# Rotary columns regrouped by halves of four maps, and differential scores in four row tiles of 32

## The chip, the cores and the metric

The kernel runs on one core of one Trainium2 chip. The metric is the device time of one execution in microseconds (us), as the median of several executions. Engines are named as in the profile: PE (TensorE, matmuls), PEld (its weight loads), DVE (VectorE), ACT (ScalarE), POOL (GpSimd) and SP (which issues the transfers from memory).

## The reference, cut to what matters

One decoder layer on 512 tokens of width 1024: a mixer (forgetting attention with 8 heads, and differential attention with rotary positions), cross-attention, a mixture of 32 experts, and a final norm. The part that the change touches is the differential attention. It has 4 heads with two maps each, and a map has 64 columns of query and 64 of key:

```python
def _rope(t, cos, sin):
    half = t.shape[-1] // 2
    t1, t2 = t[..., :half], t[..., half:]
    return jnp.concatenate([t1 * cos - t2 * sin, t2 * cos + t1 * sin], axis=-1)
...
        dq = _rope(dq.reshape(b, s, DIFF_HEADS, 2, HEAD_DIM), cos, sin)
        dk = _rope(dk.reshape(b, s, DIFF_HEADS, 2, HEAD_DIM), cos, sin)
...
        s1 = jnp.einsum('bhqd,bhkd->bhqk', q1[:, :, q0:qe], k1[:, :, :qe]).astype(jnp.float32) * scale
        s2 = jnp.einsum('bhqd,bhkd->bhqk', q2[:, :, q0:qe], k2[:, :, :qe]).astype(jnp.float32) * scale
        p1 = jax.nn.softmax(jnp.where(mask, s1, -jnp.inf), axis=-1)
        p2 = jax.nn.softmax(jnp.where(mask, s2, -jnp.inf), axis=-1)
        a = (p1 - lam * p2).astype(v.dtype)
```

## The kernel before, in words

Every float32 operand of a large matmul is split into a high and a low part (`split`, L174 to L176: an ACT copy to the high part, then a DVE subtraction for the low one), and a product takes three matmuls (high by high, low by high, high by low; L277 to L279).

The mixer is one loop over 24 iterations (L924 on). The first 16 are the forgetting attention (`Fox`, four pairs of heads by four blocks of 128 queries; block b sees 128(b+1) keys), the last 8 the differential attention (`Diff`, two groups g of four maps by four blocks). The order on each engine is that of the code (a manual schedule), and every engine works in order. An iteration does, in this order: the scores of its block on PE (`scores`), the maxima on DVE and the exponentials on ACT (`soft`), a projection unit on PE (`unit()`, 24 matmuls of 512 columns for a transposed one, some 5.5 us), the product with the values of the iteration before (`av`), the scaling (`combine`, DVE), the next half of a weight split (`W.more`), the transposes (`trans`, PE), and then the unit's evacuation `ev()` and the copies of the transposed probabilities out of PSUM (`copy`: the first of two on DVE, the second on ACT). In a Fox iteration `ev()` stands ahead of `copy`, in a Diff iteration behind it.

The rotary units (`rope_unit`) are the units of Fox iterations 6 to 9 (group 0) and 12 to 15 (group 1): query half 0, query half 1, key half 0, key half 1, of 128 columns each. A unit of before holds two whole maps. Its evacuation splits the raw result, multiplies it by the cosine, and puts a `rest` on the list `late`. `rest` runs in the next iteration behind the scores: two matmuls with a signed permutation matrix `swp` exchange the halves (L645, L646), DVE multiplies by the sine and adds, and the sum is split again.

PSUM banks come from rings (L67): two of tag "a" for units and for the exchange, four of tag "s" for scores, transposes and the key bias of a new pair (`prep`, at the end of iterations 3, 7 and 11), two of tag "y". A new tile takes the bank that was taken longest ago and waits for that tile's last reader. So the two score banks of a Fox iteration are as a rule those of the scores before. Behind a `prep` they are those of the transposes before, and a Diff iteration, which takes four banks for scores and two for transposes, has two of each.

The scores of a Diff block go by `qk_mm` (L536): two maps at a time, each on 64 rows of the array and into its own bank, so that two matmuls stand in the array side by side. Then the mask is added (L672).

Of the kernel before, what the change touches and what calls it, by code (L numbers as in the profile page):

```python
# [10 lines left out]
F32 = mybir.dt.float32  # L11
F32R = mybir.dt.float32r
# [3 lines left out]
OP = mybir.AluOpType  # L16
AX = mybir.AxisListType

P = 128
D = 1024  # L20
S = 512
# [17 lines left out]
def tile_hybrid_block(  # L39
# [5 lines left out]
    V, A, PE, G = nc.vector, nc.scalar, nc.tensor, nc.gpsimd  # L45
# [7 lines left out]
    c1 = wstack.enter_context(tc.tile_pool(name="c1", bufs=1))  # L53
    wk = wstack.enter_context(tc.tile_pool(name="wk", bufs=2))

    def page(shape, dt, name):
        return pgp.tile(list(shape), dt, name=name, tag="pg")
# [3 lines left out]
    def work(shape, dt, name, tag="w"):  # L61
        return wk.tile(list(shape), dt, name=name, tag=tag, bufs=bufs[tag])
# [10 lines left out]
    def bank(name, tag):  # L73
        return ps.tile([P, 512], F32, name=name, tag=tag, bufs={"a": 2, "s": 4, "y": 2}[tag])
# [41 lines left out]
    class Stream:  # L116
# [28 lines left out]
        def split(self, upto):  # L145

            while self.done < min(upto, 2 * len(self.spec)):
                i, j = divmod(self.done, 2)
                self.load(self.done + 1)
                _, k, n = self.spec[i]  # L150
                if j == 0:
                    self.hl[i] = [self.new.get((i, u), page)([P, k, n], F32R, f"w{u}{i}") for u in "hl"]
                hi, lo = self.hl[i]
                sl = slice(j * k // 2, (j + 1) * k // 2)
                n = k // 2 // 2 if self.done < 2 else k // 2
                for k0 in range(0, k // 2, n):
                    d = slice(sl.start + k0, sl.start + k0 + n)
                    split(hi[:, d], lo[:, d], self.raw[self.done][:, k0:k0 + n])
                self.done += 1
                self.load(self.done + 4)  # L160
# [51 lines left out]
    jp = c1.tile([P, P], F32, name="jp")  # L212
# [96 lines left out]
    def t_unit(chunk, j, evac, name):  # L309

        wh, wl = W.use(chunk, j)
        o = bank(f"{name}p{j}", "a")
        sl = slice(j * P, (j + 1) * P)
        gemm(o, KD, lambda k: wh[:, k, sl], lambda k: wl[:, k, sl], lambda k: hk(HH, k), lambda k: hk(HL, k))
        return lambda: evac(j, o)
# [113 lines left out]
    for u in range(NT):  # L429
        PE.matmul(pc[:, 8 * u:32], onesf if u else trif, logf[:, 0:NT - u].rearrange("p t c -> p (t c)"),  # L430
                  start=(u == 0), stop=(u == NT - 1), skip_group_check=True)
# [18 lines left out]
    rot = {}  # L450
# [4 lines left out]
    def rotary_angles():  # L455
        G.tensor_scalar(gcc, gcc, 0.125, None, op0=OP.mult)
        G.tensor_tensor(wr, wr, gfc[:, :, None].to_broadcast([P, KD, 36]), op=OP.mult)
        rot["sc"] = page([P, 16, P], F32, "rt")
        pf = tiny([P, NT], "pf")
        G.tensor_copy(pf, pos_i)  # L460
        ang = scratch(4)
        G.tensor_tensor(ang, pf[:, :, None].to_broadcast([P, NT, 32]), invf[:, None, :].to_broadcast([P, NT, 32]),
                        op=OP.mult)
        MAGIC = 1.5 * 2.0 ** 23
        pi_frac = Fraction(31415926535897932384626433832795028841971693993751, 10 ** 49)
        turn = pi_frac * 2
        k = scratch(0)
        G.tensor_scalar(k, ang, float(1 / turn), MAGIC, op0=OP.mult, op1=OP.add)
        G.tensor_scalar(k, k, -MAGIC, None, op0=OP.add)
        kh, kp = scratch(1), scratch(2)  # L470
        G.tensor_scalar(kh, k, 1024 * MAGIC, None, op0=OP.add)
        G.tensor_scalar(kh, kh, -1024 * MAGIC, None, op0=OP.add)
        G.tensor_tensor(k, k, kh, op=OP.subtract)
        rest = turn
        for i in range(4):
            p = cut(float(rest), 11 if i < 3 else 24)
            rest -= Fraction(p)
            for part in (kh, k):
                G.tensor_scalar(kp, part, p, None, op0=OP.mult)
                G.tensor_tensor(ang, ang, kp, op=OP.subtract)  # L480
        rot["ang"] = ang
# [55 lines left out]
    def qk_mm(banks, rows, d, j, q0, n):  # L537

        for u, w in ((0, 0), (0, 1), (1, 0)):
            for o, r0 in zip(banks, rows):  # L540
                r = slice(r0, r0 + 64)
                PE.matmul(o[:, 0:n], d[u][r, 0, j, q0:q0 + P], d[w][r, 1, j, 0:n], start=(u + w == 0), stop=False)

    class Fox:
# [15 lines left out]
        def scores(self):  # L560
            pr, b, n = self.pr, self.b, self.n
            d = fqk[pr // 2]
            self.banks = [bank(f"sf{pr}{b}{i}", "s") for i in range(2)]
            qk_mm(self.banks, [0, 64], d, pr % 2, b * P, n)
            for i in range(2):
                PE.matmul(self.banks[i][:, b * P:n], identb, maskb, start=False, stop=True)
# [51 lines left out]


    dqk = {}  # L620
    late = []
    swp = c1.tile([P, P], F32R, name="swp")

    def swap_matrix():
        for i in range(4):
            sl = slice(32 * i, 32 * i + 32)
            sg = 1.0 if i % 2 else -1.0
            V.tensor_scalar(swp[:, sl], jp[:, sl], 32.0 * sg, sg, op0=OP.is_equal, op1=OP.mult)


    def rope_unit(g, w, j):

        if g not in dqk:
            dqk[g] = [page([P, 2, 2, S], F32R, f"dqk{g}{u}") for u in "hl"]
        h, l = (t[:, w, j] for t in dqk[g])
        nm = f"r{g}{w}{j}"

        def evac(j, o):
            split(h, l, o)
            a1 = work([P, S], F32, nm + "a")  # L640
            V.tensor_tensor(a1, o, rot["cos"], op=OP.mult)

            def rest():
                sw = bank(nm + "s", "a")
                PE.matmul(sw, swp, h, start=True, stop=False)  # L645
                PE.matmul(sw, swp, l, start=False, stop=True)  # L646
                b1 = work([P, S], F32, nm + "b")
                V.tensor_tensor(b1, sw, rot["sin"], op=OP.mult)
                V.tensor_tensor(a1, a1, b1, op=OP.add)
                split(h, l, a1)  # L650

            late.append(rest)

        return t_unit((c_dq, c_dk)[w][g], j, evac, f"d{'qk'[w]}{g}")

# [2 lines left out]
    class Diff:  # L658
# [6 lines left out]
        def scores(self):  # L665
            g, b, n = self.g, self.b, self.n
            d = dqk[g]
            self.banks = [bank(f"sd{g}{b}{i}", "s") for i in range(4)]
            for j in range(2):
                qk_mm(self.banks[2 * j:2 * j + 2], [0, 64], d, j, b * P, n)  # L670
            for i in range(4):
                PE.matmul(self.banks[i][:, b * P:n], identb, maskb, start=False, stop=True)  # L672

# [240 lines left out]
    def unit():  # L914

        ev = None
        while ev is None:
            ev = units.pop()()
        return ev
# [4 lines left out]
    for n, it in enumerate(its):  # L924
        it.scores()
        it.soft()
        while late:
            late.pop(0)()
        fe = rows() if rows is not None else None
        ev = unit()  # L930
        if fe is not None:
            fe()
        fin2 = prev.av() if prev is not None else None
        if n == 1:
            swap_matrix()
        if n == 2:
            rotary_angles()
        if n == 3:
            rotary_tables()
        if n == 4:  # L940
            lam_calc()
        if n == 5:
            rotary_spread()
        if n == 7:
            dv = page([P, NT, 512], F32, "dv")
        it.combine()
        if fin is not None and isinstance(done, Diff):
            done.scale()
        W.more()
        if isinstance(it, Diff):  # L950
            ev()
            while late:
                late.pop(0)()
            ev = unit()
            W.more()
        it.trans()
        if isinstance(it, Diff):
            it.copy()
            ev()
        else:  # L960
            ev()
            it.copy()
        rows = fin
        if isinstance(it, Fox) and it.b == NT - 1 and it.pr < 3:
            Fox(it.pr + 1, 0).prep()
        if n == 15:
            YB["h"] = page([P, 4, S], F32R, "ybh")
            YB["l"] = page([P, 4, S], F32R, "ybl")
        done, prev, fin = prev, it, fin2
# [338 lines left out]
    for step in """T0 N0 U20 Q0 U21 K0 T1 N1 U30 U22 W Q1 S0 M0 K1 U23 U31 N2 T2 S1 P0 Q2 M1 U32 A0 U33 K2 T3 O0 N3 S2  # L1308
# [5 lines left out]
        f, t = step[0], int(step[1]) if len(step) > 1 else 0  # L1314
# [244 lines left out]
    for p in range(NE // 2):  # L1559
# [3 lines left out]
        h = []  # L1563
        for a in range(2):
            e = 2 * p + a
            sl = slice((2 * qi + a) * CAP, (2 * qi + a + 1) * CAP)
# [24 lines left out]
        late = more and qi == 1  # L1591
# [33 lines left out]
    def rows(o, t, j, first):  # L1625
        for u in range(2):
            PE.matmul(o, oh[:, t * P:(t + 1) * P], y2[:, u, j], start=first and u == 0, stop=(u == 1))  # L1627
# [150 lines left out]
```

## Time and profile before

| | |
|---|---|
| median of 3 runs | 1001.63 us (998.44 to 1002.61) |
| the profiled execution, its own time | 1002.39 us |
| its span, first to last instruction | 1000.7 us |
| PE busy | 960.4 us, 96% of the span |
| DVE busy, ACT busy | 473.9 us (47%), 308.7 us (31%) |
| mean granted PE clock, share of 2.4 GHz | 0.99 |
| the Fox iterations with rotary units | about 104 to 198 us from the start |
| the Diff iterations | about 189 to 297 us |
| the experts | about 500 to 985 us |

A matmul's record is longer than the distance to the next one, because matmuls overlap; for the cost on the path the distance between starts is read, not the duration. The same holds for DVE, whose records overlap by some 0.08 us.

### The profile page before, as it was taken

What the parts mean: (1) busy time and instruction counts of PE and PEld (TensorE: products, weight loads), DVE (VectorE), ACT (ScalarE), POOL (GpSimd) and SP (SyncE); (2) the same over time, 40 slices, a digit from 0 to 9 for tenths busy, and PEclk for the clock granted to TensorE, in tenths of its full rate; (3) what the DMA queues carried; (4) which work ended last, traced back from release to release, by engine and by line L of the source; (5) the groups of instructions that cost most, each with busy time, mean ns of one, the idle gap of its engine ahead of it and who ended that gap; (6) DMA issues with size and microseconds to landing.
All of it is one profiled execution on the core that took longest, in us unless ns stands there. A gap on an engine that the chain in (4) does not pass through costs nothing. (4 is left out here: it accounts for less than half of the span.)

```text
span 1000.7 us, 13844 instructions
## 1 busy us (share of the span) xinstructions
PE 960.4 (96%) x5494; PEld 639.7 (64%) x5495; DVE 473.9 (47%) x1023; ACT 308.7 (31%) x672; POOL 74.7 (7%) x189
## 2 busy tenths in 40 slices
PE   7999999999999999999799999999999999999985
PEld 6787688887878898998647446363453635436332
DVE  6555776857663657556722233433233242233335
ACT  5444444544443344435322112121111212102114
POOL 1840000001113000000200000000000000000003
PEclk9999999999999999999899999999999999999998
DMA  8211122122141337239399899999999999999902
GB/s 310 85 64 64 64 64 64 52 76 64 64 147 64 101 119 244 95 121 367 123 361 419 333 421 418 423 420 418 420 420 421 420 421 421 420 421 418 405 6 85
DMA packets 47862, 246.19 MB, mean 246 GB/s; under 512 B 4784, under 2 KB 12208, under 8 KB 23728
## 3 DMA queue, kind: packets, MB, share of 16 engines
q1 hardware_dynamic: 47648, 245.24, 62.0%
q8 instruction: 45, 0.74, 0.3%
q14 instruction: 25, 0.20, 0.1%
q10 hardware_dynamic: 144, 0.00, 0.0%
HBM read 243.13 MB, written 2.10 MB: 245 GB/s over the span
## 5 line engine op out<-in xcount | busy, mean ns | idle before, releaser
L1409 PE MATMUL gu<-gu,xg 128*64 128x512 f32 x960 | 210.5, 593 | 1.7 <-PEq L1478 1.6
L1409 PEld LDWEIGHTS gu<-gu,xg 128*64 128x64 f32 x960 | 72.9, 137 | 133.2 <-issue 123.1
L1431 PE MATMUL yd<-dn,A 128*64 128x512 f32 x472 | 110.4, 596 | 0.0
L1453 DVE TENSOR_TENSOR xr<-cb,xr 128x512 f32<-128x512 f32 x120 | 75.7, 684 | 50.8 <-PE cb L1449 50.6
L1414 DVE SCALAR_TENSOR_TENSOR A<-A,gu 128x256 f32<-128x256 f32 x32 | 13.5, 421 | 176.1 <-ACT A L1413 176.1
L176 DVE TENSOR_TENSOR wl<-wr,wh 128x1024 fp32r<-128x1024 f32 (+1 forms) x66 | 78.4, 1196 | 32.2 <-ACT wh L175 31.6
L1431 PEld LDWEIGHTS yd<-dn,A 128*64 128x64 f32 x472 | 34.9, 137 | 64.3 <-issue 63.4
L1413 ACT ACTIVATE A<-gu 128x256 f32<-128x256 f32 x32 | 12.3, 385 | 201.1 <-PE gu L1409 201.1
L175 ACT ACTIVATE wh<-wr 128x1024 fp32r<-128x1024 f32 (+1 forms) x66 | 67.0, 1026 | 7.4 <-DVE wr L142 6.4
L1449 PE MATMUL cb<-Y,ohT 128*128 128x512 f32 x240 | 67.4, 411 | 0.9
L1439 DVE SCALAR_TENSOR_TENSOR Y<-yd,ws,Y 128x512 fp32r<-128x512 f32 x32 | 23.9, 750 | 91.8 <-ACT Y L1438 89.9
L1237 PE MATMUL ga<-G,hnh 128*128 128x256 f32 x256 | 64.6, 290 | 0.2 <-DVE ge L1357 0.2
L1237 PE MATMUL ga<-G,hnl 128*128 128x256 f32 x256 | 62.7, 282 | 0.0
L1438 ACT ACTIVATE Y<-yd,ws 128x512 fp32r<-128x512 f32 x32 | 21.9, 687 | 126.9 <-PE yd L1431 126.9
L1449 PEld LDWEIGHTS cb<-Y,ohT 128*128 128x128 f32 x240 | 42.5, 191 | 12.6 <-DVE xr L1453 3.4
L1237 PEld LDWEIGHTS ga<-G,hnh 128*128 128x128 f32 x256 | 48.5, 190 | 3.1 <-issue 2.4
L1237 PEld LDWEIGHTS ga<-G,hnl 128*128 128x128 f32 x256 | 48.6, 190 | 0.6
L1383 ACT ACTIVATE xg<-ga,smc 128x256 f32<-128x256 f32 x64 | 29.9, 475 | 52.3 <-PE ga L1237 52.3
L277 PE MATMUL wop<-wh,mh 128*128 128x256 f32 x128 | 36.8, 287 | 2.0 <-DVE g L845 1.4
L278 PE MATMUL wop<-wl,mh 128*128 128x256 f32 x128 | 36.2, 283 | 0.0
L279 PE MATMUL wop<-wh,ml 128*128 128x256 f32 x128 | 36.2, 283 | 0.0
L1549 POOL MEMSET A<- 128x128 f32 x1 | 0.2, 206 | 438.2 <-PE pth L274 438.2
(609 smaller groups left out, 1888.5 us busy)
## 6 DMA issues: line engine op xcount, KB each, us to landing
gu<-in_w_gu_dram SPq DMA_DIRECT2D x120, 1024.0 KB, 11.0
dn<-in_w_dn_dram SPq DMA_DIRECT2D x55, 1024.0 KB, 16.2
wr<-in_w_inp_dram SPq DMA_DIRECT2D x40, 512.0 KB, 3.7
Z<-in_w_gu_dram SPq DMA_DIRECT2D x8, 1024.0 KB, 13.6
wr<-in_w_out_dram SPq DMA_DIRECT2D x8, 512.0 KB, 5.0
Z<-in_w_dn_dram SPq DMA_DIRECT2D x4, 1024.0 KB, 19.8
dn<-in_w_dn_dram SPq DMA_DIRECT2D x6, 512.0 KB, 12.8
x<-in_x_dram SPq DMA_DIRECT2D x2, 1024.0 KB, 11.5
```

The costliest lines, as they stand in the source:

```text
L175: A.activation(hi, src, AF.Copy)
L176: V.tensor_tensor(lo, src, hi.bitcast(F32), op=OP.subtract)
L277: PE.matmul(o, lh, rh, start=first, stop=False)
L278: PE.matmul(o, lh, rl, start=False, stop=False)
L279: PE.matmul(o, ll, rh, start=False, stop=last)
L1237: PE.matmul(o, CX[u, t // 2][:, t % 2, kb * P:(kb + 1) * P], GQ[q][:, t].rearrange("p e s -> p (e s)"), start=(first and u == "h"), stop=( ...
L1383: A.activation(XG[q][:, kb], o, AF.Copy, scale=gfc[:, kb:kb + 1])
L1409: PE.matmul(gu[64 * f:64 * f + 64, :], xg(2 * i + j), w[:, :, j, 256 * f:256 * f + 256], start=(i + j == 0), stop=(i + j == 4))
L1431: PE.matmul(y[j][64 * a:64 * a + 64, :], hT[a][:, f % 2, f // 2], w(a, f)[:, j, f % 2], start=(f == 0), stop=(f == 3))
L1439: V.scalar_tensor_tensor(yl[rows, j], y[j][rows], ws, yh[rows, j].bitcast(F32), op0=OP.mult, op1=OP.subtract)
L1449: PE.matmul(banks[j], oh[:, t * P:(t + 1) * P], y[u][:, j], start=(u == 0), stop=(u == 1))
L1453: V.tensor_tensor(xs, banks[j], xs, op=OP.add)
```

## The change

The host reorders the 1024 columns of the rotary query and key weights. Each chunk of 256 columns (four maps of 64) is laid out as the first 32 columns of the four maps, and then the second 32 columns of the four maps. A unit's 128 rows are then the first halves (j = 0) or the second halves (j = 1) of four maps, and the two halves that a rotation combines stand on the same rows of two units. The evacuation of unit 0 makes the products with cosine and sine and keeps them. That of unit 1 does the same, combines the two units, and splits the two results. `late`, `swp` and the matmuls with it are gone. A map now has 32 rows in each of two tiles. The scores run over the two halves j, over the three products, and over four maps, each on 32 rows of the array and into its own bank.

```diff
     dqk = {}
-    late = []
-    swp = c1.tile([P, P], F32R, name="swp")
...
+    rp = {}
...
         def evac(j, o):
-            split(h, l, o)
-            a1 = work([P, S], F32, nm + "a")
-            V.tensor_tensor(a1, o, rot["cos"], op=OP.mult)
-
-            def rest():
-                sw = bank(nm + "s", "a")
-                PE.matmul(sw, swp, h, start=True, stop=False)
-                PE.matmul(sw, swp, l, start=False, stop=True)
-                b1 = work([P, S], F32, nm + "b")
-                V.tensor_tensor(b1, sw, rot["sin"], op=OP.mult)
-                V.tensor_tensor(a1, a1, b1, op=OP.add)
-                split(h, l, a1)
-
-            late.append(rest)
+            c, s = (work([P, S], F32, nm + "cs"[i]) for i in range(2))
+            V.tensor_tensor(c, o, rot["cos"], op=OP.mult)
+            V.tensor_tensor(s, o, rot["sin"], op=OP.mult)
+            if j == 0:
+                rp[g, w] = c, s
+                return
+            c0, s0 = rp[g, w]
+            V.tensor_tensor(c0, c0, s, op=OP.subtract)
+            V.tensor_tensor(c, c, s0, op=OP.add)
+            for i, v in enumerate((c0, c)):
+                split(dqk[g][0][:, w, i], dqk[g][1][:, w, i], v)
...
             for j in range(2):
-                qk_mm(self.banks[2 * j:2 * j + 2], [0, 64], d, j, b * P, n)
+                for u, v in ((0, 0), (0, 1), (1, 0)):
+                    for i, o in enumerate(self.banks):
+                        r = slice(32 * i, 32 * i + 32)
+                        PE.matmul(o[:, 0:n], d[u][r, 0, j, b * P:b * P + P], d[v][r, 1, j, 0:n],
+                                  start=(j + u + v == 0), stop=False)
...
         it.soft()
-        while late:
-            late.pop(0)()
...
             ev()
-            while late:
-                late.pop(0)()
...
+    w2[:, 1536:2560] = w2[:, 1536:2560].reshape(D, 4, 4, 2, 32).transpose(0, 1, 3, 2, 4).reshape(D, 1024)
```

On DVE, at the end of Fox iteration 7 (pair 1, block 3, the unit `dq0p1`) and the start of iteration 8 the rows of before are these. `wl7` is the weight split, `pf130` the copy of the transposed probabilities, `S200` and `mx20` the next maxima.

```order
L176 TENSOR_TENSOR wl7_1208<-wr71_1049,wh7_1207 128x1024 [waits DMAHW2_49,Activation_49]
L176 TENSOR_TENSOR dqk0l_1171<-dq0p1_1259,dqk0h_1170 128x512 [waits Activation_49]
L641 TENSOR_TENSOR r001a_1311<-dq0p1_1259,rot_1113 128x512
L602 COPY pf130_1313<-tf130_1299 128x512 [waits PE_49]
L574 ISA S200_1334,mx20_1336<-sf200_1324,cb2_1317 128x128 [waits PE_49,Activation_49]
```

After:

```order
L176 TENSOR_TENSOR wl7_1203<-wr71_1044,wh7_1202 128x1024 [waits DMAHW2_49,Activation_49]
L631 TENSOR_TENSOR r001c_1296<-dq0p1_1246,rot_1108 128x512 [waits PE_49]
L632 TENSOR_TENSOR r001s_1297<-dq0p1_1246,rot_1108 128x512
L637 TENSOR_TENSOR r000c_1216<-r000c_1216,r001s_1297 128x512 [waits DVE_49]
L638 TENSOR_TENSOR r001c_1296<-r001c_1296,r000s_1217 128x512
L176 TENSOR_TENSOR dqk0l_1166<-r000c_1216,dqk0h_1165 128x512 [waits Activation_49]
L176 TENSOR_TENSOR dqk0l_1166<-r001c_1296,dqk0h_1165 128x512 [waits Activation_49]
L602 COPY pf130_1306<-tf130_1286 128x512 [waits PE_49]
L574 ISA S200_1327,mx20_1329<-sf200_1317,cb2_1310 128x128 [waits PE_49,Activation_49]
```

The copy `pf130` had two rotary operations between itself and the weight split, and now has six.

On PE, the scores of the second Diff block (iteration 17) began like this before; `sd010` to `sd013` are the four score banks:

```order
L542 MATMUL sd010_2224<-dqk0h_1170 128x256 [waits Activation_49]
L542 MATMUL sd011_2225<-dqk0h_1170 128x256 [waits Activation_49]
L542 MATMUL sd010_2224<-dqk0l_1171,dqk0h_1170 128x256
L542 MATMUL sd011_2225<-dqk0l_1171,dqk0h_1170 128x256
L542 MATMUL sd010_2224<-dqk0h_1170,dqk0l_1171 128x256
L542 MATMUL sd011_2225<-dqk0h_1170,dqk0l_1171 128x256
L542 MATMUL sd012_2226<-dqk0h_1170 128x256 [waits DVE_49]
L542 MATMUL sd013_2227<-dqk0h_1170 128x256 [waits Activation_49]
```

After:

```order
L661 MATMUL sd010_2191<-dqk0h_1165 128x256 [waits Activation_49]
L661 MATMUL sd011_2192<-dqk0h_1165 128x256 [waits Activation_49]
L661 MATMUL sd012_2193<-dqk0h_1165 128x256 [waits DVE_49]
L661 MATMUL sd013_2194<-dqk0h_1165 128x256 [waits Activation_49]
L661 MATMUL sd010_2191<-dqk0l_1166,dqk0h_1165 128x256
L661 MATMUL sd011_2192<-dqk0l_1166,dqk0h_1165 128x256
L661 MATMUL sd012_2193<-dqk0l_1166,dqk0h_1165 128x256
L661 MATMUL sd013_2194<-dqk0l_1166,dqk0h_1165 128x256
```

The matmuls that wait for the banks of the transposes before (`sd012` for a DVE copy, `sd013` for an ACT copy) stood in seventh and eighth place and now stand in third and fourth. There are 12 matmuls before the mask in a block of before, and 24 of after.

## Rows read from the trace of the kernel before

**Rows 1.** Busy time of each engine in stretches of the span, with clock and DMA.
```profile
core 0: us, PE busy (x) PEld busy (x) DVE busy (x) ACT busy (x) POOL busy (x), PEclk, DMA share, GB/s
198.00:290.00 92.00, 89.79 (x530) 74.42 (x527) 58.14 (x133) 43.84 (x114) 12.82 (x42) 1.00 0.26 86
...
580.00:620.00 40.00, 40.00 (x221) 20.97 (x221) 11.81 (x22) 6.72 (x14) 0.00 (x0) 1.00 1.02 420
```
**Rows 2.** Timeline around two exchanges: start, us, what, [idle before <-releaser].
```profile
112.83 0.48 PE L645 MATMUL r000s<-dqk0h,swp 128*128 128x512 f32 x1
...
113.63 0.19 PEld L277 LDWEIGHTS dq0p<-hh,wh 128*128 128x128 f32 x1 [0.41 <-DVE r000a L641]
...
131.20 0.48 PE L645 MATMUL r010s<-dqk0h,swp 128*128 128x512 f32 x1
...
131.75 0.39 PE L277 MATMUL dk0p<-hh,wh 128*128 128x512 f32 x1
```
**Rows 3.** Timeline, end of iteration 7 and scores of iteration 8.
```profile
120.56 0.69 DVE L176 TENSOR_TENSOR dqk0l<-dq0p,dqk0h 128x512 fp32r<-128x512 f32 x1
...
121.16 0.68 DVE L641 TENSOR_TENSOR r001a<-dq0p,rot 128x512 f32<-128x512 f32 x1
...
121.76 0.68 DVE L602 COPY pf<-tf 128x512 f32<-128x512 f32 x1
...
122.49 0.32 PE L542 MATMUL sf<-fqk1h 64*128 64x128 f32 x1 [0.30 <-DVE pf L602]
```
**Rows 4.** Timeline, end of iteration 15 and scores of iteration 16.
```profile
188.18 0.68 DVE L176 TENSOR_TENSOR dqk1l<-dk1p,dqk1h 128x512 fp32r<-128x512 f32 x1
...
190.11 0.18 PEld L542 LDWEIGHTS sd<-dqk0h 64*128 64x128 f32 x1 [0.28 <-DVE pf L602]
...
190.59 0.40 PE L672 MATMUL sd<-maskb,identb 128*128 128x128 bf16 x4
```
**Rows 5.** Timeline, iteration 14: an ACT split, the scaling on DVE, the transposes.
```profile
176.10 0.63 ACT L175 ACTIVATE dqk1h<-r101a 128x512 fp32r<-128x512 f32 x1 [0.36 <-DVE r101a L649]
...
178.17 0.75 DVE L591 TENSOR_SCALAR S<-S,ri 128x384 f32<-128x384 f32 x2
...
179.18 0.88 PE L274 MATMUL tf<-identf,S 128*128 128x128 f32 x6
```
**Rows 6.** Timeline, scores of Diff blocks: iteration 17, then 19.
```profile
204.49 0.27 ACT L710 COPY pd<-td 128x128 f32<-128x128 f32 x1 [5.41 <-PE td L274]
...
204.96 0.35 PE L542 MATMUL sd<-dqk0l,dqk0h 64*128 64x256 f32 x2
...
205.08 0.35 PE L542 MATMUL sd<-dqk0h,dqk0l 64*128 64x256 f32 x2
...
205.36 0.40 PE L672 MATMUL sd<-maskb,identb 128*128 128x128 bf16 x4
...
205.56 0.48 PE L277 MATMUL w00p<-hh,wh 128*128 128x512 f32 x1
...
232.02 0.39 PE L542 MATMUL sd<-dqk0l,dqk0h 64*128 64x512 f32 x2
...
232.25 0.39 PE L542 MATMUL sd<-dqk0h,dqk0l 64*128 64x512 f32 x2
...
233.03 0.50 PE L542 MATMUL sd<-dqk0h 64*128 64x512 f32 x1 [0.15 <-DVE pd L710]
...
233.92 0.40 PE L672 MATMUL sd<-maskb,identb 128*128 128x128 bf16 x4
```
**Rows 7.** Stretches with idle PE and the stretches behind them (columns as in rows 1).
```profile
292.00:294.80 2.80, 0.73 (x5) 0.42 (x4) 2.80 (x5) 2.02 (x3) 0.00 (x0) 1.00 0.26 61
294.00:299.00 5.00, 4.46 (x14) 3.39 (x13) 2.57 (x4) 0.69 (x1) 0.00 (x0) 0.66 0.64 207
482.00:490.00 8.00, 6.03 (x27) 4.75 (x28) 4.81 (x24) 2.12 (x6) 3.13 (x11) 0.57 0.44 183
386.50:388.20 1.70, 0.29 (x3) 0.09 (x1) 1.67 (x3) 0.00 (x0) 0.00 (x0) 1.00 1.10 352
```

More of the change, by code (lines that the diff above doesn't have):

```diff
@@ L620, in tile_hybrid_block @@
     dqk = {}
-    late = []
-    swp = c1.tile([P, P], F32R, name="swp")
[L624 to L628, printed above, removed]
+    rp = {}
     def rope_unit(g, w, j):
@@ L634, in rope_unit @@
             dqk[g] = [page([P, 2, 2, S], F32R, f"dqk{g}{u}") for u in "hl"]
-        h, l = (t[:, w, j] for t in dqk[g])
         nm = f"r{g}{w}{j}"
         def evac(j, o):
-            split(h, l, o)
-            a1 = work([P, S], F32, nm + "a")
-            V.tensor_tensor(a1, o, rot["cos"], op=OP.mult)
-            def rest():
-                sw = bank(nm + "s", "a")
-                PE.matmul(sw, swp, h, start=True, stop=False)
-                PE.matmul(sw, swp, l, start=False, stop=True)
-                b1 = work([P, S], F32, nm + "b")
-                V.tensor_tensor(b1, sw, rot["sin"], op=OP.mult)
-                V.tensor_tensor(a1, a1, b1, op=OP.add)
-                split(h, l, a1)
-            late.append(rest)
+            c, s = (work([P, S], F32, nm + "cs"[i]) for i in range(2))
[9 more added lines that the diff above has]
+                split(dqk[g][0][:, w, i], dqk[g][1][:, w, i], v)
         return t_unit((c_dq, c_dk)[w][g], j, evac, f"d{'qk'[w]}{g}")
@@ L933, in tile_hybrid_block @@
         fin2 = prev.av() if prev is not None else None
-        if n == 1:
-            swap_matrix()
         if n == 2:
```

## The prediction

> **What bounds the kernel now.** I read the page's slices first, then the busy time by stage, then the timeline of the iterations that the change touches. PE is busy 96% of the span. In the stretch of Diff iterations it works 89.79 of 92 us, and in a stretch of the experts 40.00 of 40 [rows 1]. DMA runs at 420 GB/s beside the experts, but PE waits for no transfer there: its matmuls follow each other without a gap. So PE's order is the path from the rotary units to the end, and a microsecond that PE wins or loses before 300 us is won or lost at the end. DVE and ACT count only where PE waits for them. That is seldom in before, and most of those few waits stand exactly where this change moves DVE's work.
>
> **Part 1: the exchange matmuls go.** There are 8 pairs. From the first matmul of a pair to the first one of the unit it takes 0.55 us (131.20 to 131.75). The first pair takes 0.80, because the unit behind it waits for a bank that the cosine product still reads [rows 2]. That is 7 x 0.55 + 0.80 = 4.65 us of PE time on the path. Without them the bank wait goes as well.
>
> **Part 2: DVE's work gathers in every second unit.** Over two units DVE did ten operations of 128x512 and now does eight. In before they were spread, two in each `ev()` and three in each `rest`, and a `rest` ran beside the next unit. Now `ev()` of the first unit has two, that of the second six, and in a Fox iteration all six stand ahead of DVE's `copy`. An operation takes DVE 0.60 us of its time (120.56, 121.16, 121.76), and its result is there after 0.68 [rows 3]. An ACT split takes 0.63 [rows 5]. The chain of the second unit is: cosine, sine, difference (it waits for the sine), sum, low part (it waits for ACT's copy), low part. With t0 the start of the first, the copy starts at t0 + 0.60 + 0.71 + 0.60 + 0.78 + 0.64 + 0.60 = t0 + 3.93, and in before at t0 + 1.20. So the copy lands 2.7 us later after t0. Who waits for it differs between the four second units (iterations 7, 9, 13, 15).
>
> Iteration 7: behind the key bias (`prep`) the scores of iteration 8 take the banks of the transposes. In before the second of them starts at 122.49, 0.05 behind DVE's copy [rows 3]. After: without the `rest` of iteration 6 the scaling and the weight split of iteration 7 end some 1.1 us earlier, so t0 = 119.44. The copy starts at 123.37 and lands at 124.05, and the scores go on at 124.10, 1.61 us later than before. PE is at this point 0.80 early, with its key bias done at about 120.95, so that it stands for 3.1 us. Less the exchange that stood in iteration 8, its unit starts 1.06 us later than before.
>
> Iteration 9: two more exchanges go, and PE is level at iteration 10. There the late copy pushes the maxima, and the exponentials on ACT no longer run beside a `rest`. By the same durations the scaling ends at 147.15, where PE's transposes started at 146.04: 1.1 us late. Iterations 11 and 12 keep that. Iteration 13 does the same to 14: the exchanges of 13 and 14 take 1.1 off, then the scaling ends at 180.5, where the transposes stood at 179.18 with the scaling done at 178.92 [rows 5]. PE is 1.37 late, and 0.82 after the next exchange.
>
> Iteration 15: the Diff scores of 16 need four banks, two of them those of the transposes of 15. In before their second half starts at 190.11, right behind DVE's copy, and the mask stands at 190.59 [rows 4]. After: t0 = 188.64 (behind the weight split of iteration 15), copy 192.57 to 193.25, scores from 193.3, five more steps of 0.115 and 0.31 to the mask: 194.2. Less the exchange, PE is 3.05 us later than before. It stands from about 190.05 to 193.3.
>
> The sum of parts 1 and 2 up to here, without the clock, is +3.05 us: the 4.65 us are given back, and more.
>
> **Part 3: the clock.** Both stalls (3.1 and 3.25 us) are longer than the stretch 292.0 to 294.8, in which PE was busy 0.73 of 2.80 us. Behind that one the granted clock fell to 1.2 GHz: its mean over the 5 us from 294 is 0.66, a loss of 5 x 0.34 = 1.7 us. Over the 8 us from 482, where PE is busy 6.03, it is 0.57: 3.4 us, of which some 0.7 fall into idle time, so 2.7. An idle time of 1.4 us (within 386.5 to 388.2) left it at 1.00 [rows 7]. I take the lower price for each: 2 x 1.7 = +3.4 us. The bounds are 0 and 5.4.
>
> **Part 4: four row tiles.** A block has twice as many score matmuls, and each works on 32 rows instead of 64. In before a pair takes as long as one: 0.12 us from pair to pair at 256 columns (204.96 to 205.08) and 0.23 at 512 (232.02 to 232.25) [rows 6]. I take 0.115 for 128 and 256, 0.175 for 384 and 0.235 for 512. If four go at once as two do, a block keeps its six steps, and this costs nothing. That is what I take, by the nearest row. A floor for the other end: four mask matmuls into the four banks take 0.20 us (205.36 to 205.56) [rows 6]. If a step of four can't be under 0.20, the blocks of 128 and 256 columns lose 6 x 0.085 each, those of 384 lose 6 x 0.025: 2.3 us over the eight blocks. A gain is left out, since the number of steps and of columns in each is the same.
>
> The Trainium skill, TensorE: Matmul & The Clock Gate, in Part 3, gives a measured speedup of 3.07 for four row tiles of 32 rows at 512 columns, not 4. No run here shows it. As an estimate from that page, a step of four is 1.30 of a single one, and the eight blocks lose about 2.3 us.
>
> **Part 5: four banks at once.** In before the first half of the scores runs in the two free banks while the transposes before are copied out: in iteration 17 ACT's copy lands at 204.76, the second half starts at 204.84, and the mask stands at 205.36 [rows 6]. Now the third matmul already waits. So all but the first step starts behind the copies: 204.81 + 5 x 0.115 + 0.28 = 205.67, +0.31. The same for 18 (+0.44) and 20 to 22 (+0.41, +0.35, +0.44). For 19 the wait ends at 233.03, and 233.03 + 5 x 0.235 + 0.32 = 234.5 against 233.92 [rows 6]: +0.60, and the same for 23. Sum +3.15 us. Iteration 16 is in part 2. The lower bound is 0, if the copies were to land before PE asks.
>
> The Trainium skill, TensorEngine Tiling (Array Packing), Gotcha 1: PSUM Pressure, warns of this: row tiles write to different banks and need them together. The rows above agree, in that PE waits for the copy of a bank.
>
> Off the path: the four operations that made `swp` (DVE, at 63 us) go, and no transfer is added or moved on SP or POOL. The host's reordering keeps the transfers' sizes. The work buffers (7) serve as many tiles as before, and the cosine and sine products that now live over an iteration are read before their place comes round.
>
> **The sum.** 1002.39 (the profiled execution; its span is 1000.7) + 3.05 + 3.4 + 3.15 = 1012.0. That execution stands 0.76 above the median, so I give 1011.2 for a median.
>
> **The rivals**, in the same terms.
> - The stalls come, but the clock stays at 2.4 GHz. For it: PE isn't idle throughout, since two matmuls fall into each stall. Against it: the stretch at 292 had more in it. 1011.2 - 3.4 = 1007.8.
> - Four tiles don't run at once. With a floor of 0.20 per step it is 1013.5. If only two go at once, the steps double: 2 x 6 x (0.235 + 0.175 + 0.115 + 0.115) = 7.7 us, 1018.9. For it: no instruction of before works on four row tiles. Against it: two of them cost as much as one.
> - Not slower: the late copies don't stand in the way of PE. This decides at the banks: if the scores of iterations 8 and 16 got banks that are free, PE would keep the 4.65 us and pay part 5 only: 1001.63 - 4.65 + 3.15 = 1000.1, and 997.0 if part 5 is hidden as well. For it: PE has 5.5 us of unit behind each score. Against it: before already shows PE waiting for these very copies at both places [rows 3, 4], and the order of after has the same waits (shown with the change for a Diff block).
>
> **How the numbers follow.** The forecast gets 0.56 (1006 to 1015, as the clock's price and the ends of waits vary), the clock at 2.4 GHz 0.17 (1006 to 1009), four tiles not at once 0.12 (1013 to 1019), the late copies hidden 0.15 (997 to 1003). The range from 1002 to 1016 leaves out about 0.2. About 0.5% (5 us) is what a measurement of this kernel can tell from no change: slower than 1006.6 is the forecast, nearly all of the clock rival and the tiles rival, 0.72; within it 0.23; faster than 996.6 is 0.05.
>
> **What would show it.** Right: in the profile of after a PE wait of about 3 us for `pf` (DVE) ahead of the scores at some 124 us, another ahead of the first Diff scores at some 194, a granted clock of 0.5 for some us behind each, and a PE wait of about 1 us for the scaling `S` near 147 and 180. The first unit behind the Diff scores of iteration 16 starts some 5 us later than in before. Between it and 297 another 3 us are lost, and from 300 us on all stands later by the same amount. Wrong: if the score matmuls take more than six steps a block (part 4), if the waits for `pf` are under 1 us (part 2), if the clock stays at 1.00 (part 3), or if the experts absorb the delay.

## The result, and the profile after

The kernel after takes 1011.71 us in the median of four runs (1009.94 to 1012.71), the kernel before 1002.12 beside it (998.44 to 1003.97). The ratio is 1.0098 with a 95% interval of 1.0071 to 1.0124: slower by about 1%. The profiled execution of after has a span of 1009.2 us, that of before 1000.7.

The first view gives the same stretches as [rows 1] and [rows 7]: two long ones, then each of the two stalls and the stretch behind it (columns as there).

```profile
core 0: us, PE busy (x) PEld busy (x) DVE busy (x) ACT busy (x) POOL busy (x), PEclk, DMA share, GB/s
207.00:300.00 93.00, 90.11 (x594) 73.87 (x593) 56.64 (x131) 42.72 (x112) 12.80 (x42) 1.00 0.24 80
590.00:630.00 40.00, 40.00 (x221) 20.98 (x220) 12.01 (x22) 6.71 (x14) 0.00 (x0) 1.00 1.02 419
120.50:123.80 3.30, 0.60 (x3) 0.18 (x1) 3.19 (x5) 2.58 (x5) 0.00 (x0) 1.00 0.44 148
125.00:129.00 4.00, 4.00 (x12) 3.14 (x11) 2.40 (x8) 1.83 (x5) 0.00 (x0) 0.57 0.00 0
191.00:193.80 2.80, 0.26 (x3) 0.11 (x2) 2.67 (x5) 1.71 (x3) 0.00 (x0) 0.99 0.59 187
194.00:201.00 7.00, 6.61 (x49) 6.31 (x50) 4.35 (x17) 2.56 (x9) 0.00 (x0) 0.53 0.00 0
```

Beside the experts nothing is different: 40.00 of 40 us in both. The loss lies ahead of 300 us. PE is busy 0.60 of 3.30 us and 0.26 of 2.80 us, while DVE hardly rests, and behind each stall the clock stands near 1.2 GHz (0.57 and 0.53).

Now the end of iteration 7, on three engines (timeline: start, duration, engine, line, out<-in). It answers to [rows 3].

```profile
118.04 1.22 DVE L176 TENSOR_TENSOR wl<-wr,wh 128x1024 fp32r<-128x1024 f32 x1
119.18 0.69 DVE L631 TENSOR_TENSOR r001c<-dq0p,rot 128x512 f32<-128x512 f32 x1
...
120.05 0.72 PE L557 MATMUL cbp<-cT,sel 64*128 64x512 f32 x2
...
122.36 0.56 ACT L602 COPY pf<-tf 128x512 f32<-128x512 f32 x1
...
123.10 0.68 DVE L602 COPY pf<-tf 128x512 f32<-128x512 f32 x1
...
122.98 0.32 PE L542 MATMUL sf<-fqk1h 64*128 64x128 f32 x1 [2.21 <-ACT pf L602]
123.83 0.32 PE L542 MATMUL sf<-fqk1h 64*128 64x128 f32 x1 [0.53 <-DVE pf L602]
...
124.31 0.28 PE L566 MATMUL sf<-maskb,identb 128*128 128x128 bf16 x2
```

DVE goes through its weight split and then through six rotary operations from 119.18 on, and its copy stands behind them at 123.10. PE has nothing from about 120.7 to 122.98, and its second score waits until 123.83. The same happens at iteration 16, at half clock already, where [rows 4] had the mask at 190.59:

```profile
193.80 0.47 PE L661 MATMUL sd<-dqk0h 32*128 32x128 f32 x1 [2.55 <-ACT pf L602]
194.66 0.47 PE L661 MATMUL sd<-dqk0h 32*128 32x128 f32 x1 [0.39 <-DVE pf L602]
...
196.13 0.61 PE L664 MATMUL sd<-maskb,identb 128*128 128x128 bf16 x4
```

The transposes of iterations 10 and 14 wait for the scaling; in before those of 14 came after it without a wait [rows 5]:

```profile
148.39 0.84 PE L274 MATMUL tf<-identf,S 128*128 128x128 f32 x6 [0.67 <-DVE S L591]
...
181.69 0.84 PE L274 MATMUL tf<-identf,S 128*128 128x128 f32 x6 [1.00 <-DVE S L591]
```

And a Diff block, iteration 19, beside the second half of [rows 6]. The last tile to start waits for DVE's copy, and then a step of four tiles takes 0.23 us at 512 columns (241.25 to 241.48), as a step of two does in before:

```profile
240.91 0.49 PE L661 MATMUL sd<-dqk0h 32*128 32x512 f32 x1 [0.22 <-DVE pd L702]
240.91 0.72 PE L661 MATMUL sd<-dqk0l,dqk0h 32*128 32x512 f32 x4
241.25 0.61 PE L661 MATMUL sd<-dqk0h,dqk0l 32*128 32x512 f32 x4
241.48 0.61 PE L661 MATMUL sd<-dqk0h 32*128 32x512 f32 x4
...
242.49 0.40 PE L664 MATMUL sd<-maskb,identb 128*128 128x128 bf16 x4
```

To compare kernels place by place I use the start of each iteration's mask, counted from the mask of iteration 7 in the same execution, less the same in before. The masks of iterations 7 and 8 in before, then that of 7 in after:

```profile
112.73 0.29 PE L566 MATMUL sf<-maskb,identb 128*128 128x128 bf16 x2
...
122.97 0.28 PE L566 MATMUL sf<-maskb,identb 128*128 128x128 bf16 x2
```
```profile
112.47 0.28 PE L566 MATMUL sf<-maskb,identb 128*128 128x128 bf16 x2
```

For after at iteration 8: (124.31 - 112.47) - (122.97 - 112.73) = +1.60. Positive is later than before, in us. Each row is one execution: that of e2 took 4.1 us more than the median of its kernel, that of e8 2.0 less, the others lie within 1.8 of theirs.

| mask of iteration | 8 | 9 | 15 | 16 | 17 | 20 | 23 |
|---|---|---|---|---|---|---|---|
| after | +1.60 | +2.79 | +2.74 | +5.80 | +7.62 | +9.15 | +10.78 |
| e1_rest_late | -1.06 | -1.53 | -3.27 | -3.73 | -3.84 | -2.32 | -0.71 |
| e2_no_exchange | 0.00 | +1.14 | -0.66 | -0.21 | +0.81 | +0.81 | +2.38 |
| e3_tiles32_alone | 0.00 | 0.00 | 0.00 | +0.33 | +0.69 | +2.45 | +5.36 |
| e4_filler | +1.62 | +1.18 | +1.11 | +3.52 | +4.89 | +6.41 | +7.99 |
| e5_copy_first | -1.44 | -1.87 | -0.42 | -0.98 | -1.10 | +0.43 | +3.63 |
| e6_copy_ahead | -1.05 | -1.48 | -3.27 | -3.73 | -3.85 | -1.76 | +3.40 |
| e7_av_late | -1.06 | -1.49 | -3.21 | -3.67 | -4.38 | -3.01 | +1.85 |
| e8_before_av_late | -0.01 | +0.02 | +0.01 | 0.00 | -0.27 | +1.03 | +3.01 |
| e9_av_six | -1.06 | -1.50 | -3.25 | -3.71 | -4.43 | -4.67 | -4.75 |
| e10_before_av_six | -0.01 | +0.01 | +0.01 | +0.01 | -0.26 | -1.01 | -1.13 |
| e11_two_and_two | +1.59 | +2.74 | +2.67 | +5.07 | +6.44 | +7.97 | +9.58 |
| e12_rest_late_again | -1.07 | -1.54 | -3.29 | -3.75 | -3.88 | -1.70 | +2.27 |

### The profile page after: what moved, and what is told of

Same layout as the page of the kernel before. It is cut to its first block, busy times and chain, and to the rows that moved or that the text cites. A ratio compares the mean times of both kernels' runs of the same rounds, so it can differ in the third digit from the quotient of the medians.

```text
span 1009.2 us, 13978 instructions
## 1 busy us (share of the span) xinstructions
PE 963.1 (95%) x5574; PEld 642.6 (64%) x5575; DVE 469.4 (47%) x1011; ACT 303.2 (30%) x664; POOL 73.8 (7%) x189
```

## The experiments

My theory was that the loss has three causes: the late copies ahead of the scores of 8 and 16, the half clock behind them, and the four banks that a Diff block needs at once. The rivals were that the tiles of 32 rows cost something of their own, and that it is the amount of DVE's work and not its order that PE waits for.

**The late rest.** The place of the chain's second half is changed, and the work buffers are 8 instead of 7 (the edit in short).

```diff
-            V.tensor_tensor(c0, c0, s, op=OP.subtract)
-            V.tensor_tensor(c, c, s0, op=OP.add)
-            for i, v in enumerate((c0, c)): split(...)
+            late.append(rest)      # the same four lines
...
         it.soft()
+        while late:
+            late.pop(0)()
```

> After, with the difference, the sum and the two splits of every second rotary unit issued behind the softmax maxima of the next iteration, as the kernel before issued its `rest` (the work buffers are 8 instead of 7, so that the four products live long enough). Theory (late copies of the transposes stall the scores of iterations 8 and 16, and the clock falls behind each stall): both stalls and both stretches of half clock go, the four banks' wait stays. 1002.1 - 4.65 + 3.5 (the masks' delays in iterations 17 to 23) + 0.3 (iteration 16) = 1001.3 us, some 10 below after. Rival (the 32-row tiles or the Diff blocks alone make the loss): within 2 us of after, 1010 to 1012. Rival (DVE's whole work, not its place, is what PE waits for): the wait moves to the scaling `S` of iterations 8, 10, 14; 1005 to 1008.

Measured: 1000.65 us, a ratio to before of 0.9995 (0.998 to 1.001), and when it was measured again as e12 1000.42 us, 0.9996 (0.9982 to 1.0011). The PE waits of the stretch from 100 to 310 us (total, times, longest):

```profile
PE sd L666 <- DVE pd L707: 2.2, 4, 1.2
PE tf L274 <- DVE S L591: 1.9, 2, 1.5
```

The waits for `pf` of 2.2 and 2.5 us are gone (one of 0.4 is left, at iteration 16), those for `S` are back from 3.6 to 1.9, as in before, and PE holds its lead up to iteration 17 (-3.84). From there to 23 it loses 3.1 us, with the clock at 1.00: the price of the four banks. So the place of the chain, with the clock behind it, makes the 10 us or so by which after is longer than this variant, and the amount of DVE's work, which is the same in both, makes none of it. The eighth buffer was not tried by itself, but e5 below keeps seven and loses both stalls as well.

**Part 1 alone.** The exchange is left out of before.

```diff
-                sw = bank(nm + "s", "a")
-                PE.matmul(sw, swp, h, start=True, stop=False)
-                PE.matmul(sw, swp, l, start=False, stop=True)
...
-                V.tensor_tensor(b1, sw, rot["sin"], op=OP.mult)
+                V.tensor_tensor(b1, h.bitcast(F32), rot["sin"], op=OP.mult)
```

> Before, with the exchange matmuls left out: the sine product reads the unsplit half of the same map, so the rotary part of the Diff maps is not the reference's. All DVE and ACT operations stay. It measures part 1 alone. Theory: 1002.1 - 4.65 = 997.5 us. Rival (what PE wins at the exchanges it waits for at the copies of iterations 7 and 15, where before already waits 0.3 us): a gain under 2.5 us, 999.6 to 1002.

Measured: 1000.95 us, a ratio of 0.9994 (0.9976 to 1.0013): no gain that can be told from zero. The theory fell, and the rival held. The end of iteration 15 shows why (timeline), and two stretches behind the waits (windows):

```profile
188.83 0.32 PE L542 MATMUL sd<-dqk0h 64*128 64x128 f32 x1 [0.20 <-ACT pf L602]
190.21 0.32 PE L542 MATMUL sd<-dqk0h 64*128 64x128 f32 x1 [1.05 <-DVE pf L602]
...
189.47 0.69 DVE L602 COPY pf<-tf 128x512 f32<-128x512 f32 x1
```
```profile
124.00:127.00 3.00, 3.00 (x8) 2.34 (x7) 2.14 (x7) 1.90 (x6) 0.00 (x0) 0.50 0.01 4
192.00:196.00 4.00, 4.00 (x23) 4.00 (x23) 3.07 (x10) 2.73 (x8) 0.00 (x0) 0.58 0.00 0
```

DVE's copy comes when DVE gets to it, not when PE does. At iteration 8 the 0.8 us won are lost to the wait for it (0.00 in the table), and at iteration 16 another 0.9 (from -0.66 to -0.21, where an exchange went, which is worth 0.46 from mask to mask, as from 15 to 16 in e1). Behind both waits the clock is at half, which takes 1.6 and 1.5 us (from 0.00 to +1.14 and from -0.21 to +0.81, each with 0.46 won), and it is so a third time from 246 to 250 us. This execution took 1005.05 us, 4.1 above the median, so the clock takes more in it than in most. Over all runs the half clock (the span times one less the mean granted clock) takes 11.9 us in this variant (12 runs) and 9.6 in the before beside it (23 runs), 2.3 more. In before the exchanges were a good part of what PE had to do while DVE caught up.

**Parts 4 and 5 alone.** Before, with the scores' loop of after:

```diff
             for j in range(2):
-                qk_mm(self.banks[2 * j:2 * j + 2], [0, 64], d, j, b * P, n)
+                for u, v in ((0, 0), (0, 1), (1, 0)):
+                    for i, o in enumerate(self.banks):
+                        r = slice(32 * i, 32 * i + 32)
+                        PE.matmul(o[:, 0:n], d[u][r, 0, j, b * P:b * P + P], d[v][r, 1, j, 0:n], ...)
```

> Before, with the Diff scores issued as in after: 32-row tiles, four banks in turn. The rotary units stay as they are, so the tiles multiply halves that don't belong together and the Diff maps' scores are not the reference's; the number and sizes of the matmuls are those of after. It measures parts 4 and 5 alone. Theory (a step of four costs what a step of two does; only the wait for all four banks is new): 1002.1 + 3.5 (iterations 17 to 23) + 0.3 (iteration 16) = 1005.9 us. Rival (a step of four has a price of its own): 1008 to 1010. Rival (the masks' delays are absorbed before 300 us): 1002 to 1003.

Measured: 1172.59 us, which says nothing of the scores: up to 490 us it stands some 5 us behind before, and in all it is some 163 us longer behind iteration 23, with 17305 instructions in place of 13844. That the other values in the Diff maps send tokens to other experts is the likely reason, and it is not shown. Up to iteration 23 it can be compared. It loses 0.33 at iteration 16 and 2.12 from 16 to 20. In the table it then loses 2.9 to 23, but the clock was at half from 246 to 250 us, for some 1.7 of it. Without that it is 3.7 us, as the theory has it, and no price of a tile is left over.

**The clock alone.** After, with work for PE in the two stalls:

```diff
+        if n in (8, 16):
+            d = (fqk[1] if n == 8 else dqk[0])[0]
+            z = bank(f"fill{n}", "a")
+            for i in range(10):
+                PE.matmul(z, d[:, 0, 0, 0:P], d[:, 1, 0, :], start=(i == 0), stop=(i == 9))
         it.scores()
```

> After, with ten matmuls of 128x512 that nobody reads ahead of the scores of iteration 8 and ten ahead of those of 16, into a bank of the units: 2.3 us of work each, where PE stands 2.7 and 2.9 us for the copies. Nothing else is changed, so the copies land when they did. It measures the clock by itself. Theory (the granted clock falls because PE stands): the clock stays at 1.00 in both places, and the 1.7 and 2.9 us that the half clock costs there come back: 1011.7 - 4.6 = 1007.1 us. Rival (the half clock comes from somewhere else): 1011.7 or, where the filler runs longer than the stall, 1012 to 1013.

Measured: 1008.26 us, 1.0061 (1.0042 to 1.008), 3.45 under after. Windows of the two stalls and of what follows each:

```profile
121.00:124.50 3.50, 3.18 (x15) 2.04 (x13) 3.25 (x6) 2.68 (x5) 0.00 (x0) 1.00 0.42 140
125.00:129.00 4.00, 4.00 (x19) 3.30 (x20) 2.38 (x10) 1.83 (x5) 0.00 (x0) 1.00 0.02 4
190.00:194.00 4.00, 3.21 (x25) 2.25 (x28) 3.45 (x6) 1.71 (x3) 0.00 (x0) 1.00 0.41 131
195.00:199.00 4.00, 4.00 (x24) 4.00 (x23) 3.19 (x15) 2.56 (x9) 0.00 (x0) 0.57 0.00 0
```

The first place keeps 2.4 GHz. The mask of 8 stands where it does in after (+1.62), that of 9 is 1.6 us earlier. At the second place 0.8 us of idle time is left (0.25 and 0.54), and the clock falls all the same, but for some 3.4 us instead of 7. So idle PE is what lowers the clock at the first place, and what the filler gave back of the half clock is 3.4 of those 10 us.

**The copies first.** After, in the four iterations with a second rotary unit:

```diff
-        if isinstance(it, Diff):
+        if isinstance(it, Diff) or n in (7, 9, 13, 15):
             it.copy()
             ev()
```

> After, with one thing changed: in iterations 7, 9, 13 and 15 the copies of the transposes are issued ahead of the six DVE operations and two splits of the second rotary unit, not behind them. The same work, the same units, another place. Theory (the copies' place behind the chain makes the stalls of 8 and 16): both stalls and their half clock go as in the variant with the late rest; the chain now stands ahead of the maxima of the next iteration, which may keep the waits of some 0.7 us for `S` in iterations 10 and 14. 1000.7 + 1.0 = 1001.7 us. Rival (it is the amount of DVE work in the iteration and not its order): the wait moves to the scaling of iterations 8, 10 and 14 and costs over 2 us each, 1006 to 1009.

Measured: 1004.2 us against 1000.3 for the before beside it, 1.0027 (1.0013 to 1.0041). The result lies between the two theories. The stalls of 8 and 16 are gone (-1.44, -0.98), but the six operations now stand ahead of the next maxima, and the waits for `S` grow from 1.9 to 5.0 us:

```profile
PE tf L274 <- DVE S L591: 5.0, 4, 1.7
```

At iteration 17 the lead is 2.7 us less than with the late rest (-1.10 against -3.84). A half clock from 245 to 248 us takes some 1.7 more in this execution. Ahead of the copies the chain stalls the scores, right behind them it delays the softmax; of the three places tried, only behind the next maxima is there room for it.

**Against the four banks: three attempts.** First (e6), the late rest, with DVE's copy ahead of what it queues behind in the Diff iterations; then (e7) the same with `av` of the iteration before as PE's work while the copies run; then (e8) both of these moves in before. The edit in short:

```diff
-            done.scale()           # in e6, e7, e8: behind it.copy()
         W.more()
         if isinstance(it, Diff):
-            ev()
-            ev = unit()
-            W.more()
+            ev1, ev = ev, unit()
         it.trans()
         if isinstance(it, Diff):
             it.copy()
+            fin2 = prev.av()       # e7 and e8 only
+            done.scale(); ev1(); W.more()
             ev()
```

> The variant with the late rest (1000.65 us), and in the Diff iterations DVE's copy of the transposes moved ahead of the scaling of the outputs, of the first unit's evacuation and of the second weight split. Theory (the four banks of the next scores wait for DVE's copy, which queues behind those three): the waits for `pd` ahead of the scores fall from 2.6 us to about 1, in iteration 20 by some 1.5 us, in 19, 21 and 23 by some 0.5 each: 1000.65 - 3 = 997.7 us. Rival (the 0.6 us of a copy itself and PE's run-up are what costs, not the queue ahead of it): under 1 us of gain, 999.7 to 1000.7. Rival (what is moved behind the copy is late for the next unit): slower than 1001.

> The variant before this one, and in the Diff iterations the products with the values (`av` of the iteration before) moved behind the transposes, so that PE has 0.4 to 1.7 us of work between the transposes and the next scores while the copies run. Theory (four banks at once cost PE the time in which the copies land): the waits for `pd` go nearly to nothing, the mask follows the scores' start by six steps and 0.3 us, and it gains 1.5 us more: 996 us. Rival (the transposes come earlier by as much as `av` takes and wait for the softmax in iterations 19 and 23, where the units are short): no gain, 997 to 999.

> The kernel before, with the same two moves in its Diff iterations (copy ahead, `av` behind the transposes) and nothing else. It tells whether what those moves win belongs to the tiles of 32 rows. Theory (in before only half of the scores waits, and in iterations 19 to 21 and 23 alone): the moves win some 2 us there, 1000.2 us, against 4.6 with the tiles. Rival (both have the same waits and gain the same): 997.5.

Measured beside a before of 1000.3 us: 1007.01 (1.0056, 1.0036 to 1.0075), 1003.02 (1.0024, 1.0007 to 1.0041) and 1009.41 (1.0082, 1.0062 to 1.0102). All three are slower, as the last rival of e6 has it. One place is iteration 22; from e7 (timeline):

```profile
266.49 1.23 DVE L176 TENSOR_TENSOR wl<-wr,wh 128x1024 fp32r<-128x1024 f32 x1 [1.71 <-ACT wh L175]
267.63 0.68 DVE L825 TENSOR_TENSOR g<-w02p,RT 128x512 f32<-128x512 f32 x1
...
268.37 0.79 PE L277 MATMUL w03p<-hh,wh 128*128 128x512 f32 x1 [2.47 <-DVE g L825]
```

The weight split moved behind the copy waits there for ACT, the evacuation behind it is late, and the next unit waits 2.47 us for its bank (2.42 in e6, 2.55 in e8). In e7 some seven us at half clock follow; in e6 and e8 none follow there, but e6 has them from 241 to 248 us. In iterations 19 and 23 of e7 and e8 the transposes, which come earlier by the length of `av`, wait 2.6 us for the softmax. But up to the mask of 19 the moves did what they were to do: -5.00 in e7, where the late rest alone has -2.66.

**Only what worked.** The late rest, and `av` behind the transposes in six iterations:

```diff
+        behind = isinstance(it, Diff) and n not in (19, 23)
+        if not behind:
             fin2 = prev.av() if prev is not None else None
...
             it.copy()
+            if behind:
+                fin2 = prev.av()
             ev()
```

> The variant with the late rest, and in the Diff iterations 16, 17, 18, 20, 21 and 22 the products with the values moved behind the transposes; 19 and 23, whose units are short and where the softmax is ready just in time, keep them ahead. No copy is moved. Theory (while the copies land PE does work that it has to do anyway, and nothing else comes later): the masks of 17 to 19 and 21 to 23 come earlier by 0.4 (17, 18, 22), 0.8 (19, 23) and 1.2 (21), 4.0 us in all: 5.5 us under before, a ratio of 0.9945. Rival (the transposes, which come earlier by the length of those products, wait for the softmax): under 2 us, a ratio of 0.997 to 0.999.

> The kernel before with the same move in the same six iterations. Theory (in before the scores' first half covers the copies, but for 0.5 us in 19 and 23 and 0.9 in 21): 1.9 us under before, a ratio of 0.998. Rival (the move is worth the same there): 4 us, 0.996.

> The variant with the late rest once more, beside the two kernels built on it. Theory: 1.5 us under before again, a ratio of 0.9985; the variant with the moved products must lie 4 us under it.

Measured beside a before of 1000.51 us: e9 995.58, 0.9943 (0.9922 to 0.9964); e10 998.82, 0.9976 (0.996 to 0.9992); e12 1000.42. The times of e9 and e10 are those of their theories, and e9 beats both kernels. For e12 0.9985 was forecast, which its interval (0.9982 to 1.0011) just holds. The gain of e9 over the late rest at 23 is 4.04 us, as forecast in sum (4.0), but not place by place: at iteration 19 it is 2.4 (-5.03 against -2.66), and at 21 the clock, at half from 239 to 243 us, has taken 1.7 of it. Iteration 19 in e9 (timeline):

```profile
226.25 1.06 PE L718 MATMUL zo<-dv,pd 128*128 128x128 f32 x8
227.24 0.51 PE L666 MATMUL sd<-dqk0h 32*128 32x512 f32 x4
...
228.84 0.40 PE L669 MATMUL sd<-maskb,identb 128*128 128x128 bf16 x4
```

All four first steps start together at 227.24, and the mask follows after 1.60 us; in after it was 2.93 (239.56 to 242.49).

**Two tiles, then the other two.**

```diff
+            for q in range(2):
                 for j in range(2):
                     for u, v in ((0, 0), (0, 1), (1, 0)):
-                        for i, o in enumerate(self.banks):
+                        for i in (2 * q, 2 * q + 1):
```

> After, with the score matmuls of a Diff block ordered as six steps into the first two banks and then six into the other two, so that two tiles of 32 rows run at a time and not four. Theory (a step of two costs what a step of four does): twice six steps, +7.7 us over the eight blocks, less up to 3 us of the copies' wait that the first six steps cover: 4.5 us over after, some 14 over before, a ratio of 1.014. Rival (a step of four costs nearly twice a step of two): no slower than after, a ratio of 1.006 to 1.010.

Measured: 1011.56 us, 1.0104 (1.008 to 1.0128), as long as after. The theory fell, but its rival's reason is not borne out either. Two tiles take 0.11 from step to step at 128 columns, at iteration 16 of this variant:

```profile
191.74 0.27 PE L663 MATMUL sd<-dqk0h,dqk0l 32*128 32x128 f32 x2
191.85 0.28 PE L663 MATMUL sd<-dqk0h 32*128 32x128 f32 x2
```

and four take 0.12 in the variant with the filler:

```profile
193.91 0.38 PE L661 MATMUL sd<-dqk0h 32*128 32x128 f32 x4
194.03 0.38 PE L661 MATMUL sd<-dqk0l,dqk0h 32*128 32x128 f32 x4
```

What happens stands in iteration 17:

```profile
210.81 0.39 PE L663 MATMUL sd<-dqk0h 32*128 32x256 f32 x2
...
211.15 0.29 PE L663 MATMUL sd<-dqk0h,dqk0l 32*128 32x256 f32 x2
211.17 0.45 PE L663 MATMUL sd<-dqk0h 32*128 32x256 f32 x4
...
212.14 0.40 PE L666 MATMUL sd<-maskb,identb 128*128 128x128 bf16 x4
```

From 211.17 on four matmuls start within some 0.1 us: the fourth step of the first two tiles and, by these records, the first step of the other two, which stands behind all six steps of the first two in the program. The tiles run side by side although they are issued one pair behind the other, and the mask comes 1.33 us after the first matmul, where after has 1.34 (211.38 to 212.72). So twelve steps never follow each other, whatever a step of two costs.

## Why the prediction was right

The forecast of 1011.2 us was 0.5 under the measured 1011.71, and the faster and the unchanged outcome did not come. Step by step, with the table's places:

- **The stall at 8** was predicted as 1.61 us late at the scores; the mask is 1.60 late. DVE's copy starts 3.92 behind t0, predicted 3.93. PE's waits are 2.7 us there and 2.9 at 16, predicted 3.1 and 3.25.
- **Iterations 10 and 14**: waits of 0.67 and 1.00 us, predicted 1.1 and about 1.4. At 15 after is 2.74 late; 0.82 and a half clock of 1.7 had been predicted, 2.5.
- **The stall at 16**: predicted with the mask at 194.2 and a clock price of 1.7 ahead of it, 5.3 late; measured 5.80. The rest is the half clock again: the five steps behind the copy take 0.21 each and not 0.115.
- **The exchange** was priced at 0.55 us by the distance of two starts; from mask to mask it is worth 0.46 (e1, 15 to 16). Part 1's sum is some 0.6 too high.
- **The clock** was the term with the least ground, and the value was somewhat low: 1.7 behind the first stall (from +1.60 to +2.79, with 0.46 won) and about 3 behind the second (0.53 over 7 us), against 1.7 each.
- **The four tiles** cost nothing, as taken. The Trainium skill, TensorE: Matmul & The Clock Gate, Part 3, has 3.07 instead of 4 for them; the steps of 0.23 us with two and with four do not show that loss, and the measurement decides.
- **The four banks**: predicted 3.15 for iterations 17 to 23, of which 0.31 belongs to 17 itself and 2.84 to the rest. Measured from 17 to 23 are 3.16 in after (from +7.62 to +10.78) and 3.13 with the late rest, and 0.36 at 17 in e3: about 3.5.

At 23 after is thus 10.8 us late, where the terms add up to 9.6. By the end of the span 8.5 are left. Of the difference 0.26 lie ahead of the mask of 7, which stands at 112.47 and not at 112.73. Around 490 us the clock is at half for some 6.8 us in both kernels, and at most 0.6 us come back there. The larger part, 1.7 us, comes back near the end: behind a wait of 2.62 us for `dg`, which both have, the clock falls in before and not in after (windows, before and then after).

```profile
956.00:964.00 8.00, 7.67 (x20) 4.24 (x20) 3.51 (x7) 1.19 (x2) 0.00 (x0) 0.79 0.01 2
```
```profile
966.00:974.00 8.00, 7.48 (x28) 4.01 (x28) 5.17 (x9) 1.19 (x2) 0.00 (x0) 1.00 0.01 3
```

Nothing here ties this to the change: of the two executions of the late rest e1 has that half clock, at 955 us, and e12 has not. Over all runs the half clock takes 13.9 us in after (4 runs) and 9.6 in before (23 runs), 4.3 more, where 3.4 was forecast. So of the 9.6 us between the medians some 5.3 are left for the other terms, an estimate, where 6.2 was forecast. That the total came out within 0.5 us is in part luck: the mechanism held at every place, but errors of some tenths to 0.9 us stand against each other.

One sentence did not hold: that a microsecond which PE wins ahead of 300 us is won at the end. Part 1 by itself wins nothing (e2), since DVE's copies set the time at 8 and 16. The sum escaped this because it followed DVE's chain from t0 and not PE's matmuls; the late rest takes the copies out of the way as the rival of 1000.1 supposes, and it measures 1000.65 and 1000.42.

## What to carry to other kernels

Before taking work from an engine that looks like the bound, look for the places where it already waits a few tenths of a microsecond: there the other engine's queue sets the time, and what is won ahead of them is lost to that wait and to the clock behind it. When a chain gathers on one engine, ask what stands behind it in that queue and who waits for that; against their place behind the next maxima, the same operations cost about 10 us ahead of the copies and about 3 ahead of the maxima, the clock's part included. When more banks are needed at once, give PE work that it must do anyway between the last use of the banks and the next.

## What the runs showed of the hardware that I had not expected

The same program has the half clock at a place in one execution and not in another. In the two executions of the late rest PE waits 0.42 and about 1.2 us for the copies ahead of iteration 20, alike, and this is the stretch from 241 on, first of e1, then of e12:

```profile
241.00:249.00 8.00, 6.95 (x61) 6.22 (x62) 5.35 (x18) 2.89 (x15) 0.00 (x0) 1.00 0.22 66
```
```profile
241.00:249.00 8.00, 7.30 (x41) 6.22 (x42) 4.99 (x18) 2.20 (x9) 0.00 (x0) 0.57 0.20 66
```

That is worth 3 us in the table (-0.71 and +2.27 at 23). The two executions end alike all the same (spans of 999.1 and 998.6 us), since e1 has more of the half clock later: 480 to 487 and 954.5 to 958 us, where e12 has 484 to 487.5 alone. So a given wait has no fixed price in clock: 1.4 us of idle time left it at 1.00 in [rows 7], and behind 0.8 it fell in e4. The half clock lasted about 3.4 us at most places and about 7 at several (from 194 in after, from 241 in e12). What decides that, no run here shows. The scatter of one kernel goes with it: in the last 24 runs of before the shortest span, 995.9 us, has a mean granted clock of 0.994, and the longest, 1002.7, has 0.988.

And row tiles that do not share rows ran side by side in both orders in which their matmuls were issued here, interleaved (after) and one pair behind the other (e11). Between row tiles PE's matmuls thus did not start strictly in the order of the code.
